# GpSimd in place of the sync queue for the turned blocks of h, with a reordered start and halved last sums, in a two-layer encoder kernel

## Chip, cores and metric

The kernel runs on one core of a Trainium2 chip. The metric is the device time of one execution in microseconds; lower is better. A core has five engines that run side by side, each through its own list of instructions in order: TensorE (PE; its weight loads are PEld), VectorE (DVE), ScalarE (ACT), GpSimd (POOL) and the sync engine (SP), which issues transfers. They meet through semaphores.

## The reference

Two layers over x of 256 rows by 1024 columns, in float32:

```python
for i in range(DEPTH):                       # 2
    h = rmsnorm(x, ffn1_norm[i])
    x = x + 0.5 * swiglu(h, ffn1_w_gate[i], ffn1_w_up[i], ffn1_w_down[i])
    h = rmsnorm(x, mix_norm[i])
    q_s, k_s, v_s, q_m = split(h @ w_in[i])
    o_m = memory_attention(q_m, *kv(rmsnorm(mem, mem_norm[i]) @ w_mem_kv[i]))
    o_s = chunked_rel_attention(...) if i % 2 == 0 else diff_attention(...)   # rotary in layer 1
    x = x + concat(o_s, o_m) @ w_out[i]
    h = rmsnorm(x, ffn2_norm[i])
    x = x + 0.5 * swiglu(h, ffn2_w_gate[i], ffn2_w_up[i], ffn2_w_down[i])
```

`swiglu(h, g, u, d)` is `(silu(h @ g) * (h @ u)) @ d`, with 2816 hidden columns. So there are four feed-forward blocks, two before and two behind a mixer.

## The kernel before

**Numbers.** Every large product is made of three TensorE products on float32r parts: high times high, low of the weights times high of the activations, high times low (`dense`, L378 to L392, products at L383, L386, L389). So each weight is split: ACT copies it to `hi` (L302), DVE subtracts to get `lo` (L314).

**Weights.** They come in chunks of 1 MB, 128 partitions by 2048 numbers. `loader` issues them on the sync queue (L270) into three `raw` buffers, `split_hi` and `split_lo` split a chunk in four quarters of 512 columns into four pairs of `hi` and `lo` buffers, and a `raw` buffer is free again when DVE has made the last `lo` of its chunk. A chunk of gate and up weights holds 512 rows by 256 columns of each; two chunks make a group, and 11 groups a feed-forward block.

**Activations.** The 256 rows are two row blocks (`tb` 0 and 1) of 128. `prep_half` turns half of a row block of x (`hf`): four transposes on TensorE (L396) into `xtp`, the gain times it on DVE (`y`, L427), the high part on ACT (`xh`, L430), the low part on DVE (`xl`, L432). The norm's factor is applied after the product.

**A feed-forward block** (`ffn`). For each group, 48 products give `gu` for both row blocks, in PSUM. `evac` makes silu on ACT (`sil`, L491), the product `h` on DVE (L494), and turns h: DVE transposes blocks of 32 by 32 (`hb`, L503), one transfer of 256 KB writes them to DRAM (`hd`, L508), and four of 64 KB read them back with the blocks in their new places (`hr`, L514). ACT and DVE then split `hr` into `ht` (L521, L523). The second half multiplies `ht` with the down weights into four PSUM sums (`acc`); `finish` adds them to x (L466). In the very last block it stores the sum to `out` (L473).

**What sets the order.** `Flow` simulates the engines in Python while the kernel is written out: each step waits for a modelled time or a free buffer, and the order in which the steps come due is the order in which instructions stand on each engine. A changed delay can so move instructions on every engine. On the chip each engine then runs its list in order and waits where an input isn't there; in particular a transfer on the sync queue that waits for its source holds up all transfers behind it.

**The start.** The sync queue loads the first gains and half of x's first row block, the first chunk in four pieces, then the other halves of x between weights. TensorE runs some `warm` products meanwhile. Four `start` threads turn the halves of x at written times (L1279).

Of the kernel before, what the change touches and what calls it, by code (L numbers as in the profile page):

```python
# [17 lines left out]
ALU = mybir.AluOpType  # L18
AX = mybir.AxisListType

P = 128
# [6 lines left out]
KT = D // P  # L28
# [114 lines left out]
def kernel(  # L143
# [10 lines left out]
    nc = tc.nc  # L154
    PSUM = bass.MemoryType.PSUM
    NRAW, NHL, NT2 = 3, 4, 19
    flow = Flow()
# [27 lines left out]
    def load_x(tb, hf):  # L185
        nc.sync.dma_start(out=xs[tb][:, hf * 512:(hf + 1) * 512],
                          in_=x[0, tb * P:(tb + 1) * P, hf * 512:(hf + 1) * 512])

    load_x(0, 0)

    ident = const.tile([P, P], F32, name="ident")
    make_identity(nc, ident)
# [56 lines left out]
    chunks = []  # L249
    raw_left = [NRAW]  # L250
    hl_left = [NHL]
    dma_free = [2.3]
    LAT = 1.5
    at = [0]

# [7 lines left out]
    def loader():  # L263
        for i, c in enumerate(chunks):
            yield lambda: raw_left[0] > 0
            raw_left[0] -= 1
            c.raw = wraw.tile([P, 2048], F32, tag="raw", name=f"raw{i}")
            dma_free[0] = max(dma_free[0], flow.now)
            for j, (dst, src) in enumerate(c.parts):
                nc.sync.dma_start(out=dst(c.raw), in_=src)  # L270
                dma_free[0] += 2.9 / len(c.parts)
                if j == 1 and i < 2:
                    c.early = dma_free[0] + LAT
                    if i:
                        load_x(1, 1)
                        dma_free[0] += 0.7
            c.arrive = dma_free[0] + LAT
            if i == 0:
                load_x(1, 0)
                load_x(0, 1)  # L280
                dma_free[0] += 1.4
            if i > 4 and late_done[0] < len(late_loads):
# [35 lines left out]
    def k4(t):  # L318
        return t.rearrange("p (k n) -> p k n", k=4)
# [140 lines left out]
    def finish(acc, tb, xt, gc, half):  # L460
        for hf in range(2):
            sl = slice(hf * 512, (hf + 1) * 512)
            yield lambda: acc.t[tb][hf] is not None
            yield acc.t[tb][hf]
            if half:
                nc.vector.scalar_tensor_tensor(out=xs[tb][:, sl], in0=acc.ps[tb][hf], scalar=0.5, in1=xs[tb][:, sl],  # L466
                                               op0=ALU.mult, op1=ALU.add)
            else:
                nc.vector.tensor_add(xs[tb][:, sl], acc.ps[tb][hf], xs[tb][:, sl])
            banks.give()  # L470
            yield flow.dve(512)
            if xt is None:
                nc.sync.dma_start(out=out[0, tb * P:(tb + 1) * P, sl], in_=xs[tb][:, sl])  # L473
            else:
                yield from prep_half(xt, tb, hf, gc)


    def ffn(l, nm, xt, gc_next):
# [3 lines left out]
        def evac(g, ps, end):  # L482


            hb = None
            for tb in range(2):
                yield lambda: end[tb] is not None and xt.rt[tb] is not None
                yield end[tb]
                yield g2.has(3)
                sil = g2.take([P, 256], F32, "sil")  # L490
                nc.scalar.activation(sil, ps[tb][:, 0:256], AF.Silu, scale=xt.r[tb])  # L491
                yield flow.act(256)
                h = g2.take([P, 256], F32, "h")
                nc.vector.scalar_tensor_tensor(out=h, in0=ps[tb][:, 256:512], scalar=xt.r[tb], in1=sil,  # L494
                                               op0=ALU.mult, op1=ALU.mult)
                t = flow.dve(256, 0.06)
                g2.give()
                banks.give()
                if hb is None:
                    hb = g2.take([P, 4, 2, 2, 32], F32, "hb")  # L500
                yield t
                for f in range(2):
                    nc.vector.transpose(out=hb[:, :, f, tb, :], in_=h[:, f * P:(f + 1) * P])  # L503
# [4 lines left out]
            nc.sync.dma_start(out=hd.rearrange("a i b x -> (a i) (b x)"), in_=hb.rearrange("p b f t j -> p (b f t j)"))  # L508
            yield flow.now + 3.0
            g2.give()  # L510
            yield g2.has()
            hr = g2.take([P, 4, 2, 2, 32], F32, "hr")
            for b in range(4):
                nc.sync.dma_start(out=hr[32 * b:32 * b + 32].rearrange("p a f t j -> p a (f t j)"),  # L514
                                  in_=hd[:, :, b, :].rearrange("a i x -> i a x"))
# [5 lines left out]
            nc.scalar.copy(out=hi, in_=src)  # L521
            yield flow.act(512)
            nc.vector.tensor_sub(lo, src, hi.bitcast(F32))  # L523
            t = flow.dve(512)
            g2.give()
            hts[g], htt[g] = ht, t

        for g, ids in enumerate(plan[l, nm, "gu"]):
            flow.until(banks.has(2))
            ps = [bank(f"gu{tb}", (P, 512)) for tb in range(2)]  # L530
            end = [None, None]
            flow.spawn(evac(g, ps, end))
            order = [(tb, c) for tb in range(2) for c in range(2)] if g == 0 and (l, nm) != (0, 1) else \
                    [(tb, c) for c in range(2) for tb in range(2)]
            for tb, c in order:
                for k in range(4):
                    kk = 4 * c + k
                    t = dense(ps[tb], xt.h[tb][:, kk, :], xt.l[tb][:, kk, :], lambda: xt.t[tb][kk], ids[c], k,
                              lambda w: k4(w)[:, k, :], kk == 0, kk == KT - 1)
                if c == 1:  # L540
                    end[tb] = t
        flow.until(banks.has(4))
        acc = Acc()
# [706 lines left out]
    xt = Xt()  # L1250

    def start_gain():
        tp = bank("gps0")
        nc.tensor.transpose(out=tp[:, 0, :16], in_=g1row, identity=ident[:16, :16])
        yield flow.pe(T_TR)
        nc.vector.tensor_copy(gcol[:, 0:16], tp[:, 0, :16])
        banks.give()
        flow.dve(16)
        warm(2)
        yield 5.0  # L1260
        warm(6)

    def start(tb, hf, t):
        yield t
# [11 lines left out]
    flow.spawn(start_gain())  # L1276
    for tb in range(2):
        for hf in range(2):
            flow.spawn(start(tb, hf, (3.75, 8.2, 7.4, 10.4)[2 * tb + hf]))  # L1279
    flow.spawn(gain_columns())  # L1280
    flow.spawn(rope_setup(), idle=True)
    flow.spawn(lambda_setup())
# [58 lines left out]
```

## Time and profile before

| | us |
|---|---|
| median of 3 runs | 974.63 |
| lowest, highest | 974.41, 975.08 |
| profiled execution | 975.12 |
| its span, from the first to the last instruction | 973.3 |
| busy in the span: PE, PEld, DVE, ACT, POOL | 964.6, 791.3, 675.7, 542.4, 60.1 |
| sync-queue issues: weights gate, up and down, hd, hr | 90, 90, 44, 44, 176 |

A line of the profile names the source line, the engine, the operation, what it writes and reads, and how many there are. A wait names who waited and whose semaphore ended it last. A matmul's end is modelled, so busy TensorE isn't TensorE at its peak; two products that follow each other overlap, and it is the distance of their starts that counts. "SPq" is the sync queue; the duration of a transfer on it is that of its issue, not of the bytes.

### The profile page before, as it was taken

What the parts mean: (1) busy time and instruction counts of PE and PEld (TensorE: products, weight loads), DVE (VectorE), ACT (ScalarE), POOL (GpSimd) and SP (SyncE); (2) the same over time, 40 slices, a digit from 0 to 9 for tenths busy, and PEclk for the clock granted to TensorE, in tenths of its full rate; (3) what the DMA queues carried; (4) which work ended last, traced back from release to release, by engine and by line L of the source; (5) the groups of instructions that cost most, each with busy time, mean ns of one, the idle gap of its engine ahead of it and who ended that gap; (6) DMA issues with size and microseconds to landing.
All of it is one profiled execution on the core that took longest, in us unless ns stands there. A gap on an engine that the chain in (4) does not pass through costs nothing.

```text
span 973.3 us, 13393 instructions
## 1 busy us (share of the span) xinstructions
PE 964.6 (99%) x4576; PEld 791.3 (81%) x4576; DVE 675.7 (69%) x1485; ACT 542.4 (56%) x1159; POOL 60.1 (6%) x65
## 2 busy tenths in 40 slices
PE   9999999999999999999999999999999999999998
PEld 7888888887777888888888888888787788888886
DVE  6776675887777866666476676644989886676641
ACT  6554544766685655445445555443677764555540
POOL 0000000022210000000000000000344100000000
PEclk9999999999999999999999999999999999999999
DMA  9989766475525567887648887764641369788641
GB/s 289 306 242 270 257 225 206 162 260 173 174 87 173 163 209 223 242 263 242 235 124 252 250 252 237 253 207 136 207 140 50 125 199 284 235 251 254 226 130 44
DMA packets 164447, 200.90 MB, mean 206 GB/s; under 512 B 9433, under 2 KB 140058, under 8 KB 164378
## 3 DMA queue, kind: packets, MB, share of 16 engines
q1 hardware_dynamic: 164378, 200.04, 65.5%
q8 instruction: 36, 0.59, 0.3%
q14 instruction: 33, 0.27, 0.1%
HBM read 187.42 MB, written 12.58 MB: 205 GB/s over the span
## 4 chain that ended last, share of the span: by engine, by line
PE 91%; DVE 5%; ACT 1%; DMA 1%; issue 0%; SPq 0%; ACTq 0%
PE gu L383 16%; PE gu L386 16%; PE gu L389 16%; PE acc L386 9%; PE acc L389 9%; PE acc L383 9%; PE pj L389 3%; PE pj L383 3%; PE pj L386 3%; DVE lo L314 2%; PE xtp L396 1%; PE S L983 1%; PE AV L1064 1%; PE kv L389 1%; PE kv L386 1%; PE kv L383 1%
## 5 line engine op out<-in xcount | busy, mean ns | idle before, releaser
L314 DVE TENSOR_TENSOR lo<-raw,hi 128x512 fp32r<-128x512 f32 x656 | 416.5, 684 | 161.5 <-ACT hi L302 161.3
L302 ACT CAST hi<-raw 128x512 fp32r<-128x512 f32 x656 | 365.4, 618 | 241.3 <-PE gu L389 117.9
L389 PE MATMUL gu<-hi,xl 128*128 128x512 f32 x704 | 274.3, 390 | 0.0
L383 PE MATMUL gu<-hi,xh 128*128 128x512 f32 x704 | 274.1, 389 | 0.0
L386 PE MATMUL gu<-lo,xh 128*128 128x512 f32 x704 | 274.0, 389 | 0.0
L389 PEld LDWEIGHTS gu<-hi,xl 128*128 128x128 f32 x704 | 132.2, 188 | 27.5
L383 PEld LDWEIGHTS gu<-hi,xh 128*128 128x128 f32 x704 | 132.2, 188 | 27.3
L386 PEld LDWEIGHTS gu<-lo,xh 128*128 128x128 f32 x704 | 132.2, 188 | 27.2
L383 PE MATMUL acc<-hi,ht 128*128 128x512 f32 x352 | 137.7, 391 | 0.0
L386 PE MATMUL acc<-lo,ht 128*128 128x512 f32 x352 | 137.3, 390 | 0.2 <-DVE lo L314 0.2
L389 PE MATMUL acc<-hi,ht 128*128 128x512 f32 x352 | 137.4, 390 | 0.0
L386 PEld LDWEIGHTS acc<-lo,ht 128*128 128x128 f32 x352 | 66.1, 188 | 14.1 <-DVE lo L314 0.7
L389 PEld LDWEIGHTS acc<-hi,ht 128*128 128x128 f32 x352 | 66.1, 188 | 13.7
L383 PEld LDWEIGHTS acc<-hi,ht 128*128 128x128 f32 x352 | 66.1, 188 | 13.5
L523 DVE TENSOR_TENSOR ht<-hr,ht 128x512 fp32r<-128x512 f32 x44 | 30.3, 688 | 55.0 <-ACT ht L521 55.0
L521 ACT CAST ht<-hr 128x512 fp32r<-128x512 f32 x44 | 27.1, 617 | 69.5 <-DMA hr<-hd 69.5
L389 PE MATMUL pj<-hi,xl 128*128 128x512 f32 x160 | 64.6, 404 | 0.0
L386 PE MATMUL pj<-lo,xh 128*128 128x512 f32 x160 | 63.6, 398 | 0.0
L383 PE MATMUL pj<-hi,xh 128*128 128x512 f32 x160 | 63.6, 398 | 0.0
L491 ACT ACTIVATE sil<-gu,xr 128x256 f32<-128x256 f32 x88 | 41.4, 470 | 17.5 <-PE gu L389 17.5
L503 DVE STREAM_TRANSPOSE hb<-h 128x128 f32<-128x128 f32 x176 | 44.1, 289 | 1.2
L494 DVE SCALAR_TENSOR_TENSOR h<-gu,xr,sil 128x256 f32<-128x256 f32 x88 | 42.2, 480 | 1.6
(167 smaller groups left out, 806.5 us busy)
## 6 DMA issues: line engine op xcount, KB each, us to landing
raw<-in_ffn_w_down_dram SPq DMA_DIRECT2D x44, 1024.0 KB
raw<-in_ffn_w_gate_dram SPq DMA_DIRECT2D x86, 512.0 KB
raw<-in_ffn_w_up_dram SPq DMA_DIRECT2D x86, 512.0 KB
raw<-in_w_in_dram SPq DMA_DIRECT2D x32, 512.0 KB
hd<-hb SPq DMA_DIRECT2D x44, 256.0 KB
hr<-hd SPq DMA_DIRECT2D x176, 64.0 KB
raw<-in_w_out_dram SPq DMA_DIRECT2D x8, 1024.0 KB
raw<-in_w_mem_kv_dram SPq DMA_DIRECT2D x4, 1024.0 KB
```

What stands on the lines that cost most here:

```text
L302: nc.scalar.copy(out=c.hi[:, sl], in_=c.raw[:, sl])
L314: nc.vector.tensor_sub(c.lo[:, sl], c.raw[:, sl], c.hi.bitcast(F32)[:, sl])
L383: nc.tensor.matmul(out=ps, lhsT=xh, rhs=wh, start=start, stop=False)
L386: nc.tensor.matmul(out=ps, lhsT=xh, rhs=wl, start=False, stop=False)
L389: nc.tensor.matmul(out=ps, lhsT=xl, rhs=wh, start=False, stop=stop)
L396: nc.tensor.transpose(out=dst, in_=src, identity=flip if flipped else ident)
L491: nc.scalar.activation(sil, ps[tb][:, 0:256], AF.Silu, scale=xt.r[tb])
L494: nc.vector.scalar_tensor_tensor(out=h, in0=ps[tb][:, 256:512], scalar=xt.r[tb], in1=sil, op0=ALU.mult, op1=ALU.mult)
L503: nc.vector.transpose(out=hb[:, :, f, tb, :], in_=h[:, f * P:(f + 1) * P])
L521: nc.scalar.copy(out=hi, in_=src)
L523: nc.vector.tensor_sub(lo, src, hi.bitcast(F32))
L983: nc.tensor.matmul(out=ss[e][:, pr, :nk], lhsT=q[rows, pr, :], rhs=k[rows, pr, :], start=i == 0, stop=i == len(passes) - 1)
```

## The change

Four edits:

1. The transfers `hd` and `hr` are issued by GpSimd instead of the sync queue.
2. At the start, x's second row block's first half is loaded ahead of the weights, both second halves behind the first chunk; the planned times of `start` change from (3.75, 8.2, 7.4, 10.4) to (3.75, 9.2, 4.6, 9.9); six `warm` products become ten, in pairs.
3. In the first group, the products go through the eight slices of the inner dimension and take both row blocks at each, where they took four slices of one row block and then of the other. All other groups keep their order.
4. The last feed-forward block adds its sums in 256-column pieces, and stores them in turn from the sync queue and from ACT.

```diff
     load_x(0, 0)
+    load_x(1, 0)
...
-    dma_free = [2.3]
+    dma_free = [4.0]
...
                 if j == 1 and i < 2:
                     c.early = dma_free[0] + LAT
-                    if i:
-                        load_x(1, 1)
-                        dma_free[0] += 0.7
...
             if i == 0:
-                load_x(1, 0)
                 load_x(0, 1)
+                load_x(1, 1)
...
+            if xt is None:
+                for q in range(2):
+                    qs = slice(hf * 512 + q * 256, hf * 512 + q * 256 + 256)
+                    nc.vector.scalar_tensor_tensor(out=xs[tb][:, qs], in0=acc.ps[tb][hf][:, q * 256:q * 256 + 256],
+                                                   scalar=0.5, in1=xs[tb][:, qs], op0=ALU.mult, op1=ALU.add)
+                    yield flow.dve(256)
+                    (nc.scalar if q else nc.sync).dma_start(out=out[0, tb * P:(tb + 1) * P, qs], in_=xs[tb][:, qs])
+                banks.give()
+                continue
...
-            nc.sync.dma_start(out=hd.rearrange("a i b x -> (a i) (b x)"), in_=hb.rearrange("p b f t j -> p (b f t j)"))
+            nc.gpsimd.dma_start(out=hd.rearrange("a i b x -> (a i) (b x)"), in_=hb.rearrange("p b f t j -> p (b f t j)"))
...
-                nc.sync.dma_start(out=hr[32 * b:32 * b + 32].rearrange("p a f t j -> p a (f t j)"),
+                nc.gpsimd.dma_start(out=hr[32 * b:32 * b + 32].rearrange("p a f t j -> p a (f t j)"),
...
+            if (l, nm) == (0, 1) and g == 0:
+                order = [(tb, kk) for kk in range(KT) for tb in range(2)]
...
-        yield 5.0
-        warm(6)
+        for t in (5.0, 5.6, 6.2, 6.8, 7.4):
+            yield t
+            warm(2)
...
-            flow.spawn(start(tb, hf, (3.75, 8.2, 7.4, 10.4)[2 * tb + hf]))
+            flow.spawn(start(tb, hf, (3.75, 9.2, 4.6, 9.9)[2 * tb + hf]))
```

Where instructions stand now. On TensorE at the start of the program, before (`x_85` and `x_86` are x's first and second row block, `gu_147` and `gu_148` their sums):

```order
L396 MATMUL xtp<-ident,x_85 128x128 x4
L1269 MATMUL warm<-ident 128x128 x6
L396 MATMUL xtp<-ident,x_86 128x128 x4
L383 MATMUL gu_147<-hi_166,xh_126 128x512
L386 MATMUL gu_147<-lo_167,xh_126 128x512
L396 MATMUL xtp<-ident,x_85 128x128 x4
L389 MATMUL gu_147<-hi_166,xl_128 128x512
L383 MATMUL gu_147<-hi_166,xh_126 128x512
```

and in the changed kernel, at the same place (its source lines differ by a few):

```order
L394 MATMUL xtp<-ident,x_85 128x128 x4
L394 MATMUL xtp<-ident,x_86 128x128 x4
L1277 MATMUL warm<-ident 128x128 x10
L381 MATMUL gu_147<-hi_178,xh_126 128x512
L384 MATMUL gu_147<-lo_179,xh_126 128x512
L387 MATMUL gu_147<-hi_178,xl_128 128x512
L394 MATMUL xtp<-ident,x_85 128x128 x4
L381 MATMUL gu_148<-hi_178,xh_127 128x512
L384 MATMUL gu_148<-lo_179,xh_127 128x512
L394 MATMUL xtp<-ident,x_86 128x128 x4
L387 MATMUL gu_148<-hi_178,xl_129 128x512
```

The first transposes of the second row block went ahead of the warm products, and the last transposes of both stand within the first two triples. On DVE at the start, before:

```order
L427 TENSOR_TENSOR y<-xtp,gcol 128x512
L432 TENSOR_TENSOR xl_128<-y,xh_126 128x512
L314 TENSOR_TENSOR lo_167<-raw_110,hi_166 128x512 x3
L427 TENSOR_TENSOR y<-xtp,gcol 128x512
L314 TENSOR_TENSOR lo_167<-raw_110,hi_166 128x512
```

and in the changed kernel:

```order
L425 TENSOR_TENSOR y<-xtp,gcol 128x512 x2
L430 TENSOR_TENSOR xl_128<-y,xh_126 128x512
L430 TENSOR_TENSOR xl_129<-y,xh_127 128x512
L312 TENSOR_TENSOR lo_179<-raw_111,hi_178 128x512 x4
L425 TENSOR_TENSOR y<-xtp,gcol 128x512 x2
```

Two instructions of the second row block, y and xl, now stand ahead of the first weight split. On the sync queue in the first block, before, around the first group's h:

```order
L508 DMA hd<-hb 128x512
L270 DMA raw_369<-in_ffn_w_gate_dram 128x4x256
L270 DMA raw_369<-in_ffn_w_up_dram 128x4x256
L285 DMA grow<-in_ffn_norm_dram 16x128
L514 DMA hr<-hd 32x4x128 x4
L270 DMA raw_400<-in_ffn_w_gate_dram 128x4x256
```

and in the changed kernel on POOL, from its first norm factors on:

```order
L401 TENSOR_TENSOR xr<-v,nhalf 128x1 x2
L512 DMA hd<-hb 128x512
L518 DMA hr<-hd 32x4x128 x4
L512 DMA hd<-hb 128x512
L518 DMA hr<-hd 32x4x128 x4
```

On POOL the transfers of all 11 groups of a block follow each other with no other instruction between them; on the sync queue only weights, x and small constants are left. Apart from these moves, the lists of all engines are the same in both kernels from the first block's fourth group to the last sums.

More of the change, by code (lines that the diff above doesn't have):

```diff
@@ L471, in finish @@
             yield flow.dve(512)
[L472 to L475, printed above, removed]
+            yield from prep_half(xt, tb, hf, gc)
     def ffn(l, nm, xt, gc_next):
@@ L532, in ffn @@
             flow.spawn(evac(g, ps, end))
[L533 to L540, printed above, removed]
+            if (l, nm) == (0, 1) and g == 0:
+                order = [(tb, kk) for kk in range(KT) for tb in range(2)]
+            elif g == 0:
+                order = [(tb, kk) for tb in range(2) for kk in range(KT)]
+            else:
+                order = [(tb, 4 * c + k) for c in range(2) for tb in range(2) for k in range(4)]
+            for tb, kk in order:
+                c, k = kk // 4, kk % 4
+                t = dense(ps[tb], xt.h[tb][:, kk, :], xt.l[tb][:, kk, :], lambda: xt.t[tb][kk], ids[c], k,
+                          lambda w: k4(w)[:, k, :], kk == 0, kk == KT - 1)
+                if kk == KT - 1:
                     end[tb] = t
```

## The prediction

> **What bounds the kernel now.** I read the page first, then the busy times by stretch, then who waits on TensorE and on the sync queue, and last the timeline at both ends. The page's engine line and six stretches (columns: length, then busy time and instruction count of PE, PEld, DVE, ACT, POOL, the granted clock, the DMA share and GB/s):
>
> ```profile
> PE 964.6 (99%) x4576; PEld 791.3 (81%) x4576; DVE 675.7 (69%) x1485; ACT 542.4 (56%) x1159; POOL 60.1 (6%) x65
> 0.00:9.00 9.00, 6.71 (x33) 6.26 (x34) 2.81 (x6) 4.08 (x7) 1.21 (x10) 1.00 0.70 215
> 12.30:160.00 147.70, 147.70 (x654) 121.99 (x653) 106.39 (x236) 82.33 (x161) 1.11 (x2) 1.00 0.84 262
> 330.00:480.00 150.00, 150.00 (x664) 124.24 (x663) 96.92 (x216) 75.34 (x148) 0.94 (x1) 1.00 0.77 238
> 510.00:660.00 150.00, 150.00 (x663) 124.25 (x662) 96.23 (x190) 76.31 (x144) 0.86 (x1) 1.00 0.78 239
> 690.00:780.00 90.00, 87.82 (x502) 69.29 (x502) 81.25 (x184) 64.69 (x182) 30.89 (x27) 1.00 0.40 130
> 800.00:950.00 150.00, 150.00 (x663) 124.20 (x663) 96.10 (x189) 76.29 (x145) 0.00 (x0) 1.00 0.73 228
> ```
>
> In the four feed-forward stretches TensorE is busy without a gap, at one product per 0.226 us (150 us by 663), while DVE has a third of its time free and ACT half. The h blocks are turned in exactly these stretches. TensorE loses time only at the start, around layer 1's mixer (690 to 780) and at the end. The waits on TensorE say the same, and those on the sync queue and on ACT show what the moved transfers hold up today (waiter, releaser, us in total, times, longest):
>
> ```profile
> PE xtp L396 <- DMA x<-in_x_dram: 0.9, 1, 0.9
> PE acc L386 <- DVE lo L314: 0.2, 1, 0.2
> SPq L270 <- DVE lo L314: 367.1, 115, 18.5
> SPq L508 <- DVE hb L503: 167.9, 39, 6.1
> SPq L514 <- DMA hd<-hb: 34.0, 25, 5.3
> ACT ht L521 <- DMA hr<-hd: 69.5, 26, 6.2
> ```
>
> The sync queue does stand still 201.9 us in all for the h transfers, with weight loads queued behind them. But no TensorE wait names a weight that landed late in those stretches: the loads have slack. How much, the counts of weight quarters split by DVE (L314) and of the middle products started (L386) give, each quarter serving two of these, at 420 us, the leanest place in them:
>
> ```profile
> 0.00:420.00 420.00, 180.76 (x284) 1.00 0.69 215
> ...
> 0.00:420.00 420.00, 216.87 (x553) 104.00 (x554) 1.00 0.69 215
> ```
>
> 284 less 553/2 is 7.5 quarters ahead; a quarter is six products, 1.36 us, so TensorE could run 10.2 us there with no new weight. That cover hides most of this change.
>
> **The h transfers, moved to GpSimd.** 44 groups lose 5 sync-queue issues each. The two rows of durations are min/median/max in ns; below them, the first group on the timeline, and the dearest group of POOL instructions today (busy us, mean ns):
>
> ```profile
> L514 SPq DMA_DIRECT2D hr<-hd x176: 312/427/1487, 30.8 to 916.5; - x176
> L508 SPq DMA_DIRECT2D hd<-hb x44: 338/345/506, 26.0 to 913.1; - x44
> ...
> 26.04 0.42 SPq L508 DMA_DIRECT2D hd<-hb  x1
> 30.77 1.77 SPq L514 DMA_DIRECT2D hr<-hd  x4
> 35.59 0.62 ACT L521 CAST ht<-hr 128x512 fp32r<-128x512 f32 x1 [2.89 <-DMA hr<-hd]
> ...
> L403 POOL TENSOR_TENSOR hf<-v,nhalf 128x8 f32<-128x8 f32 (+1 forms) x20 | 30.9, 1544 | 106.1 <-DVE v L401 88.0 <-DVE sst L450 18.0
> ```
>
> The sync queue is freed of 176 times 0.427 and 44 times 0.345, 90 us of issuing, besides the 201.9 us of waiting. Gain on the path: nothing, since its weight loads then wait for the next thing, a raw buffer that DVE frees (the 367.1 us row), and TensorE already has them early. No stretch without a TensorE gap can become shorter by it, and layer 1's mixer holds no h transfer.
>
> The cost sits on the other side. What waits now on POOL is hd for hb, and hr for hd's landing; queued behind are only the next group's five transfers, since POOL computes nothing in these stretches but one or two reciprocal roots (0 to 2 instructions in the four rows above). What waits for POOL is ACT's ht, and behind it in ACT's order the next weight splits. The trace shows no GpSimd transfer, so I bound its issue by the sync queue's 0.35 us from below and POOL's dearest group, 1.54 us, from above, and take 1.0 between them; below the sync queue's price a gain would again find nothing to shorten. A group then holds POOL for 1.0 for hd, its landing (26.46 to 30.77, 4.3 us, behind a megabyte of weights in the same queue; shorter if the new queue is served in turn), and 4.0 for hr: 9.3 us, within the 10.9 us that TensorE gives a group (48 products of 0.226). POOL keeps up; ht comes 2.8 us later than today (5.0 of issues for 2.2), and the 10.2 us of lead hide that. Without that lead it would cost up to 2.8 us in each of 44 groups. I put 0, with ends 0 and the first rival below.
>
> One row speaks against so calm a view: DVE is busy 96.92 us of the 150 in the second stage, mostly with instructions of 0.68 us, beside every one of these issues. The Trainium skill (SBUF — State Buffer, SBUF: two separate sides) warns that GpSimd cannot write a transfer's descriptors while DVE holds the port that the two share, as it does in certain copy modes. The same page clears a two-input subtraction, which is most of DVE's work here, of holding the write side; no run here shows either. If the warning held for all of DVE's work, each issue would wait out the instruction in hand, and the sum would change as in the second rival; by the rows alone it stays at 0.
>
> **The start.** Columns: start, duration, engine, line, what.
>
> ```profile
> 4.59 1.06 PE L396 MATMUL xtp<-ident,x 128*128 128x128 f32 x4
> 5.68 0.69 DVE L427 TENSOR_TENSOR y<-xtp,gcol 128x512 f32<-128x512 f32 x1 [1.83 <-PE xtp L396]
> 6.41 0.62 ACT L430 CAST xh<-y 128x512 fp32r<-128x512 f32 x1 [4.19 <-DVE y L427]
> 6.93 2.18 ACT L302 CAST hi<-raw 128x512 fp32r<-128x512 f32 x4
> 7.06 0.69 DVE L432 TENSOR_TENSOR xl<-y,xh 128x512 fp32r<-128x512 f32 x1 [0.68 <-ACT xh L430]
> 7.67 1.89 DVE L314 TENSOR_TENSOR lo<-raw,hi 128x512 fp32r<-128x512 f32 x3
> 8.59 0.66 PE L396 MATMUL xtp<-ident,x 128*128 128x128 f32 x4 [0.94 <-DMA x<-in_x_dram]
> 9.01 0.48 PE L383 MATMUL gu<-hi,xh 128*128 128x512 f32 x1
> 9.33 0.40 PE L386 MATMUL gu<-lo,xh 128*128 128x512 f32 x1
> 9.60 0.42 PEld L396 LDWEIGHTS xtp<-ident,x 128*128 128x128 f32 x4 [0.32 <-DMA x<-in_x_dram]
> 11.95 0.60 PE L396 MATMUL xtp<-ident,x 128*128 128x128 f32 x4
> 15.37 0.39 PE L389 MATMUL gu<-hi,xl 128*128 128x512 f32 x1
> ```
>
> Today the first product stands behind transposes that wait for x of the second row block (8.59). The 24th and last product of the first chunk starts at 15.37, and from about 12.6 on there is no gap, so this is where a gain would show. In the new order that x block lands before the weights, and the block's y, xh and xl go ahead of the first split. Worked through with the rows' spacing (0.21 us between early transposes, 0.60 between DVE's and 0.52 between ACT's 512-wide instructions): the four extra transposes take 0.85 us, so the second y starts at 6.53 and ends at 7.22; its xh on ACT runs 7.25 to 7.87; hi follows, 7.77 to 8.39; on DVE the second xl runs 7.9 to 8.6 and the first lo to 9.2. The first lo product comes at 9.25, against 9.33. So the wait for x (0.9 us) goes and a longer chain through DVE and ACT stands in its place. After it: the third product at 9.48, four transposes of the next x block (the same bytes lie ahead of it as today, so it lands by 9.60) to 10.13, two products, the last x block's transposes at 10.6 (a block later: 8.59 to 9.60 is one block) to 11.03, then products alone: the 24th at 11.03 + 18 x 0.226 = 15.1. Gain 0.26 us.
>
> Ends: 0.7 us gained if lo goes as soon as hi is there, 8.5; 0.9 us lost if the last x block still lands at 11.9 as today. Later chunks are covered: each quarter of the first chunk is now used by both row blocks in turn, so demand for splits is slower, and the second chunk is wanted at 15.3.
>
> **The end.** The last sums, their store, and a 128x256 sum of the same kind (page, mean 480 ns):
>
> ```profile
> 969.57 0.69 DVE L466 SCALAR_TENSOR_TENSOR x<-acc,x 128x512 f32<-128x512 f32 x1 [3.39 <-PE acc L389]
> 970.28 0.33 SPq L473 DMA_DIRECT2D out_dram<-x  x1
> ...
> 971.00:972.00 1.00, 0.00 (x0) 0.00 (x0) 0.00 (x0) 0.00 (x0) 0.00 (x0) 1.00 0.70 262
> ...
> L494 DVE SCALAR_TENSOR_TENSOR h<-gu,xr,sil 128x256 f32<-128x256 f32 x88 | 42.2, 480 | 1.6
> ```
>
> The last 256 KB flow within 971 to 972 (262 GB/s), then come the receipt and the span's end at 973.3. Two half sums end by 969.57 + 0.40 + 0.48 = 970.45 (if they overlap by 0.08, as DVE's back-to-back instructions do), 0.19 later than the one; the last store is then half as large, 0.5 us less, with the other half already under way. Net 0.3 gained, 0.5 if the sums cost no more than the one. ACT issues no transfer today; at the sync queue's 0.33 the gain stands, at its slowest hr issue, 1.49, it is a loss of 0.9; I take 0.33, the like transfer. The six other half sums hide beside TensorE, as the four stores do now.
>
> **The sum.** 0 - 0.26 - 0.3 is -0.56 us. The profiled execution took 975.12 us (973.3 of span and 1.8 around it), 0.05% above the median of 974.63; taken from its own time that gives 974.56, and on the median's footing 974.1 us. The measurement can tell about 0.2%, 1.95 us, from no change, so this is no change.
>
> **The rivals.** *POOL falls behind by its own price (slower).* If a GpSimd issue costs 1.6 us, just over POOL's dearest row, a group takes 1.6 + 4.3 + 6.4 = 12.3 us of POOL against 10.9 of TensorE; it slips 1.4 us a group, 14 us by a stage's eleventh, past the lead of 10.2 us in the leanest stage: some 4 us of TensorE gap, 978.1 us, and steeply more beyond. The deciding point is 1.3 us an issue, where a group fills 10.9. For it: no row bounds the issue. Against: the dearest row is arithmetic, and the landing should shrink in a queue without weights. Chance 0.05.
>
> *DVE holds GpSimd off (slower).* An issue of 1.0 that first waits out a DVE instruction of 0.68 takes 1.68; a group takes 5 x 1.68 + 4.3 = 12.7, slips 1.8, 18 us by the eleventh, 8 past the leanest lead: 982 us. For it: DVE is busy 65% of the stretch. Against: a third of the issues would find it idle, which brings the mean to 1.44 and the slip to 6 us, inside the lead. Chance 0.04.
>
> *Earlier weights shorten layer 1's mixer, or the start gains its full 0.7 and more (faster).* The chain of waits holds one weight transfer at the mixer's end:
>
> ```profile
> 767.22 6.30 DMA raw<-in_ffn_w_up_dram
> ```
>
> Landing 3 us sooner would give 971.1. Against: no h transfer is queued there, and the buffer that it waits for comes from DVE. Chance 0.11 for all that ends under 972.7.
>
> *The end or start turns (slower).* Both worst ends, 0.9 and 0.9, give 976.4, still no change; with something around the span for the two new queues it could pass 976.6. Chance 0.03.
>
> **How the numbers follow.** The forecast, within 0.2%, has the remaining 0.77; slower has 0.05 + 0.04 + 0.03. The range is the forecast's: down by the start's further 0.45, the end's 0.2 and the runs' own spread of 0.35 to 973.0, up by the start's worst end against the forecast (1.15) and half of the end's (1.2) to 975.8, since both worst together are unlikely; the far rivals stay outside.
>
> **What would show it.** Right: the four feed-forward stretches of the new trace keep a PE without gaps, L314's count stays 6 quarters or more ahead, sync-queue waits for hb are gone and those for lo grow; the first lo product at about 9.2 and the 24th at about 15.1. Wrong: a TensorE wait for lo or ht in those stretches, POOL issues above 1.3 us, or a first chunk that ends after 15.8; a gain above 2 us would have to appear between 690 and 780, where I expect none.

## The result and the profile after

The changed kernel takes 1037.11 us (median of 6 runs, 1035.75 to 1041.80) against 974.77 us for the kernel before in the same comparison (6 runs, 974.41 to 975.08). The ratio is 1.0646, with an interval of 1.0626 to 1.0666: 62.3 us slower, where 974.1 us and no change were forecast. The profiled execution of the changed kernel has a span of 1034.9 us.

The engine line of the page after, and the first feed-forward stretch (columns as in the prediction); below them the counts of weight quarters split by DVE (L312) and of middle products started (L384) up to 160 us:

```profile
PE 985.7 (95%) x4584; PEld 796.9 (77%) x4584; DVE 670.2 (65%) x1489; ACT 534.8 (52%) x1159; POOL 181.0 (17%) x285
12.30:160.00 147.70, 140.53 (x605) 114.36 (x603) 87.87 (x192) 69.17 (x139) 28.66 (x52) 0.98 0.73 222
...
0.00:160.00 160.00, 63.93 (x102) 0.98 0.73 225
...
0.00:160.00 160.00, 80.31 (x204) 38.77 (x204) 0.98 0.73 225
```

Before, TensorE was busy through the whole of 12.3 to 160 us and started 654 products in it. Now it starts 605 in the same time: 49 fewer, and at 0.226 us each that is 11 us lost by 160 us alone. The busy time hides much of this (140.53 of 147.70), the count of products shows it. DVE and ACT are less busy than before in this stretch, and the DMA share fell from 0.84 to 0.73. So something waits, everywhere a little, and no engine is saturated. The lead of weights is gone: 102 quarters less 204/2 is 0, where the prediction asked for 6 or more.

A part of the loss shows in the granted clock. In the changed kernel it is 0.5 in four stretches (79.4 to 86.2, 195.5 to 202.3, 683.6 to 687.0 and 932.8 to 939.6 us), each behind gaps in TensorE's work. The 46 products that start in them stand 0.43 us apart (median) instead of 0.226, an estimate of at most 9 us. The kernel before has no such stretch until its last product is done.

Who waits, from the waits of the changed kernel (waiter, releaser, us in total, times, longest):

```profile
POOL hd L512 <- DVE hb L507: 337.0, 44, 10.8
ACT ht L525 <- DMA hr<-hd: 317.0, 44, 10.5
DVE ht L527 <- ACT ht L525: 251.7, 43, 9.4
PE acc L381 <- ACT hi L300: 16.4, 10, 5.2
PE gu L381 <- ACT hi L300: 7.9, 6, 2.2
PE acc L384 <- DVE lo L312: 6.1, 11, 0.7
PE gu L384 <- DVE lo L312: 5.9, 9, 0.7
```

ACT's `ht` waited 69.5 us in 26 groups before; it waits 317.0 us in all 44 now, and DVE's `ht` another 251.7 us behind it. TensorE waits for weight halves `hi` and `lo`, which the prediction named as the sign that it is wrong. Yet POOL isn't the late one: it waits 337.0 us for `hb`, in every group. Everybody waits for somebody else in the same circle, and the circle has to be followed. The price of an issue, and how long the bytes take from issue to landing (line, engine, operation, count, busy us, mean ns; then count, KB each, median us):

```profile
L518 POOL DMA_DIRECT2D hr<-hd x176 | 95.7, 550 | 124.8 <-ACT hi L300 59.8
L512 POOL DMA_DIRECT2D hd<-hb x44 | 25.0, 569 | 337.0 <-DVE hb L507 337.0
L312 DVE TENSOR_TENSOR lo<-raw,hi 128x512 fp32r<-128x512 f32 x656 | 412.7, 682 | 37.9 <-ACT hi L300 37.3
...
hd<-hb POOLq DMA_DIRECT2D x44, 256.0 KB, 2.5
hr<-hd POOLq DMA_DIRECT2D x176, 64.0 KB, 6.0
```

Issues cost 0.55 and 0.57 us, near the lower end of the prediction's bounds and not the 1.0 taken. DVE's instructions take what they took. But a piece of `hr`, a quarter of the bytes of `hd`, lands 6.0 us after its issue. The page before gives no landing for the sync queue.

**The circle.** DVE's list around one group, the same in both kernels (the names are those of the changed one; `h` of the group's second row block, then the low half of `ht` of the group before, then `hb`):

```order
L498 SCALAR_TENSOR_TENSOR h<-gu_5054,xr,sil 128x256
L527 TENSOR_TENSOR ht<-hr,ht 128x512
L507 STREAM_TRANSPOSE hb<-h 128x4x32 x2
```

DVE takes its list in order, so the `hb` of group g can't be made before the `ht` of group g-1 is. That `ht` needs ACT's `ht`, that needs `hr` to land, that needs `hd` to land, and that needs the `hb` of group g-1. The chain starts at an `hb` and comes back to the next `hb`. One turn in the changed kernel, on the timeline (start, duration, engine, line, what, idle time before and who ended it):

```profile
602.32 0.50 DVE L507 STREAM_TRANSPOSE hb<-h 128x128 f32<-128x128 f32 x2
603.11 0.56 POOL L512 DMA_DIRECT2D hd<-hb  x1 [8.10 <-DVE hb L507]
606.12 2.17 POOL L518 DMA_DIRECT2D hr<-hd  x4 [2.44 <-ACT hi L300]
608.43 0.48 DVE L498 SCALAR_TENSOR_TENSOR h<-gu,xr,sil 128x256 f32<-128x256 f32 x1
614.37 0.62 ACT L525 CAST ht<-hr 128x512 fp32r<-128x512 f32 x1 [7.79 <-DMA hr<-hd]
615.02 0.69 DVE L527 TENSOR_TENSOR ht<-hr,ht 128x512 fp32r<-128x512 f32 x1 [6.11 <-ACT ht L525]
615.63 0.50 DVE L507 STREAM_TRANSPOSE hb<-h 128x128 f32<-128x128 f32 x2
```

`h` of the second row block is ready at 608.91, and its `hb` waits until 615.63 for the `ht` that stands ahead of it, though `hb` uses nothing of it. From `hb` to `hb` is 615.63 - 602.32 = 13.31 us, and the legs fill it without slack: 0.79 to the issue of `hd`, 0.56 for that, 2.45 until POOL issues `hr`, 2.17 for the four issues, 6.08 until ACT can read `hr`, 0.65 and 0.61 through ACT and DVE. TensorE needs 10.88 us a group (48 products of 0.226).

The same turn before:

```profile
592.81 0.50 DVE L503 STREAM_TRANSPOSE hb<-h 128x128 f32<-128x128 f32 x2
593.33 0.34 SPq L508 DMA_DIRECT2D hd<-hb  x1
595.43 1.75 SPq L514 DMA_DIRECT2D hr<-hd  x4
602.24 0.61 ACT L521 CAST ht<-hr 128x512 fp32r<-128x512 f32 x1
603.69 0.50 DVE L503 STREAM_TRANSPOSE hb<-h 128x128 f32<-128x128 f32 x2
```

From `hb` to `hb` is 10.88 us, TensorE's own period, and `ht` has no waiting time in brackets: the circle is there, but it is shorter than the period and has some slack. Over the 44 groups the chain from the end of `hb` to the start of ACT's `ht` is 11.9 us on average after and 9.2 before, ACT's own order and waiting included. With the 1.8 us of `ht` on ACT, `ht` on DVE and `hb` (0.62, 0.69, 0.50) the circle is 13.7 us after. Before it is at most 11.0, next to the period, and the transfers alone are done earlier than that: the last packet of `hr` is through 8.0 us after `hb` on average, and ACT waits for `hr` in only 26 groups.

An estimate of the loss from this: 13.3 - 10.9 = 2.4 us in each of the 11 groups of a block is 26 us; the lead of 10.2 us that the prediction read off covers part of it; 16 us are left, and four blocks make 64 us. Measured: 62.3. That the two come so near is partly luck. From the first gate product to the last down product the four blocks are 20.8, 9.5, 15.4 and 16.5 us longer than before; these add up to the loss, but no block is the average one.

### The profile page after: what moved, and what is told of

It is laid out like the page before. It is cut to its first block, busy times and chain, and to the rows that moved or that the text cites. A ratio compares the mean times of both kernels' runs of the same rounds, so it can differ in the third digit from the quotient of the medians.

```text
span 1034.9 us, 13443 instructions
## 1 busy us (share of the span) xinstructions
PE 985.7 (95%) x4584; PEld 796.9 (77%) x4584; DVE 670.2 (65%) x1489; ACT 534.8 (52%) x1159; POOL 181.0 (17%) x285
## 5 line engine op out<-in xcount | busy, mean ns | idle before, releaser
L312 DVE TENSOR_TENSOR lo<-raw,hi 128x512 fp32r<-128x512 f32 x656 | 412.7, 682 | 37.9 <-ACT hi L300 37.3
L300 ACT CAST hi<-raw 128x512 fp32r<-128x512 f32 x656 | 360.8, 617 | 80.9 <-PE gu L387 30.3
L381 PE MATMUL gu<-hi,xh 128*128 128x512 f32 x704 | 276.9, 393 | 7.9 <-ACT hi L300 7.9
L384 PE MATMUL gu<-lo,xh 128*128 128x512 f32 x704 | 276.9, 393 | 5.9 <-DVE lo L312 5.9
L527 DVE TENSOR_TENSOR ht<-hr,ht 128x512 fp32r<-128x512 f32 x44 | 30.4, 692 | 251.7 <-ACT ht L525 251.7
L525 ACT CAST ht<-hr 128x512 fp32r<-128x512 f32 x44 | 27.3, 620 | 317.0 <-DMA hr<-hd 317.0
L384 PEld LDWEIGHTS gu<-lo,xh 128*128 128x128 f32 x704 | 133.3, 189 | 36.9 <-DVE lo L312 8.8
L381 PE MATMUL acc<-hi,ht 128*128 128x512 f32 x352 | 140.8, 400 | 16.4 <-ACT hi L300 16.4
L384 PE MATMUL acc<-lo,ht 128*128 128x512 f32 x352 | 140.2, 398 | 6.1 <-DVE lo L312 6.1
L387 PE MATMUL acc<-hi,ht 128*128 128x512 f32 x352 | 139.0, 395 | 0.0
L518 POOL DMA_DIRECT2D hr<-hd x176 | 95.7, 550 | 124.8 <-ACT hi L300 59.8
L384 PEld LDWEIGHTS acc<-lo,ht 128*128 128x128 f32 x352 | 67.0, 190 | 24.6 <-DVE lo L312 10.8
L512 POOL DMA_DIRECT2D hd<-hb x44 | 25.0, 569 | 337.0 <-DVE hb L507 337.0
L387 PEld LDWEIGHTS acc<-hi,ht 128*128 128x128 f32 x352 | 67.0, 190 | 13.3
L384 PE MATMUL pj<-lo,xh 128*128 128x512 f32 x160 | 63.6, 398 | 0.0
L401 POOL TENSOR_TENSOR hf<-v,nhalf 128x8 f32<-128x8 f32 (+1 forms) x20 | 30.9, 1545 | 108.5 <-DVE v L399 88.3
```

What stands on the lines that cost most here:

```text
L300: nc.scalar.copy(out=c.hi[:, sl], in_=c.raw[:, sl])
L312: nc.vector.tensor_sub(c.lo[:, sl], c.raw[:, sl], c.hi.bitcast(F32)[:, sl])
L381: nc.tensor.matmul(out=ps, lhsT=xh, rhs=wh, start=start, stop=False)
L384: nc.tensor.matmul(out=ps, lhsT=xh, rhs=wl, start=False, stop=False)
L387: nc.tensor.matmul(out=ps, lhsT=xl, rhs=wh, start=False, stop=stop)
L401: nc.gpsimd.tensor_tensor(out=dst, in0=v[:, :n], in1=nhalf[:, :n], op=ALU.pow)
```

## The experiments

The theory under test: the loss comes from the length of this circle (call it the ring) alone; what lengthens it costs, what shortens it or opens it doesn't. The rivals: GpSimd as an issuer is too slow or disturbs the engines beside it, whatever the order; the wait that counts is that of ACT, which splits the weights; the other three edits have a part in it.

**Which edit.** The first kernel is the one before with only `hd` and `hr` moved; the second is the changed kernel with only these two moved back, the same lines the other way round.

```diff
-            nc.sync.dma_start(out=hd.rearrange("a i b x -> (a i) (b x)"), in_=hb.rearrange("p b f t j -> p (b f t j)"))
+            nc.gpsimd.dma_start(out=hd.rearrange("a i b x -> (a i) (b x)"), in_=hb.rearrange("p b f t j -> p (b f t j)"))
...
-                nc.sync.dma_start(out=hr[32 * b:32 * b + 32].rearrange("p a f t j -> p a (f t j)"),
+                nc.gpsimd.dma_start(out=hr[32 * b:32 * b + 32].rearrange("p a f t j -> p a (f t j)"),
```

Expected of the first: 

> Edit: the kernel before with the first edit alone, hd and hr issued from GpSimd; start, first products and last sums as before. Ring theory: on DVE the list reads h of group g, ht of group g-1, hb of group g, so hb(g) waits for ht(g-1), which waits for the transfers that hb(g-1) started; on GpSimd that ring is 11.6 us of transfers and 1.8 of ACT and DVE work, 13.4 us against the 10.9 that TensorE takes for a group, so all of the loss is here: 1036 to 1038 us. Queue theory (the GpSimd queue's own traffic slows weights or DVE): also about 1037. Rival, the new start and last sums carry the loss: 975.

Expected of the second: 

> Edit: the changed kernel with hd and hr back on the sync queue, so the reordered start and the halved last sums alone. Ring and queue theories alike: no loss, 974.1 us by the prediction's own sum for the start and the end (0.26 and 0.3 gained on 974.8 to 974.6). Rival, these edits carry the loss: above 1000.

Measured: 1039.55 us (ratio 1.0636, 1.0612 to 1.0661), a little above the 1036 to 1038 expected, and 975.49 us (0.9995, 0.9986 to 1.0004). The transfers carry the whole loss, the other edits none of it.

**Opening the ring by order.** Nothing is made faster here: `ht` is planned 4 us later, so that it stands behind the next `hb` on DVE. From the changed kernel, ahead of `ht`:

```diff
-            yield flow.now + 4.0
+            yield flow.now + 8.0
```

Expected: 

> Edit: the changed kernel, transfers on GpSimd, with the planned delay between hr and ht raised from 4 to 8 us, which puts ht of group g-1 behind hb of group g on DVE and behind two more weight splits on ACT. Ring theory: the ring is cut, a chain of 13.4 us is then hidden, 974 to 977 us. Queue theory: the traffic is the same, so the loss stays, 1030 or more.

Measured: 974.22 us (973.74 to 974.35), ratio 0.9982 (0.9973 to 0.9991). 62.9 us come back with every transfer still on GpSimd at the same issue price. DVE's list and the timeline of this kernel:

```order
L498 SCALAR_TENSOR_TENSOR h<-gu_5054,xr,sil 128x256
L312 TENSOR_TENSOR lo_5147<-raw_5049,hi_5146 128x512
L507 STREAM_TRANSPOSE hb<-h 128x4x32 x2
L312 TENSOR_TENSOR lo_5147<-raw_5049,hi_5146 128x512
L527 TENSOR_TENSOR ht<-hr,ht 128x512
```

```profile
593.48 0.56 POOL L512 DMA_DIRECT2D hd<-hb  x1 [5.28 <-DVE hb L507]
597.35 2.17 POOL L518 DMA_DIRECT2D hr<-hd  x4 [3.31 <-ACT hi L300]
603.57 0.50 DVE L507 STREAM_TRANSPOSE hb<-h 128x128 f32<-128x128 f32 x2
604.76 0.62 ACT L525 CAST ht<-hr 128x512 fp32r<-128x512 f32 x1 [1.50 <-DMA hr<-hd]
605.41 0.69 DVE L527 TENSOR_TENSOR ht<-hr,ht 128x512 fp32r<-128x512 f32 x1 [0.77 <-ACT ht L525]
...
12.30:160.00 147.70, 147.70 (x652) 121.99 (x651) 106.23 (x235) 82.92 (x160) 31.39 (x57) 1.00 0.84 261
```

The chain from `hd` to `ht` is as long as ever (593.48 to 604.76, 11.3 us). But `hb` now comes before `ht`, the next turn has begun by then, and TensorE is back at 652 products without a gap.

**On which engine the ring closes.** The edit above moves `ht` on ACT too. This one moves only DVE's half, and leaves ACT to wait for `hr` where it did. From the changed kernel, between the two halves of `ht`:

```diff
-            yield flow.act(512)
+            yield flow.act(512) + 1.5
```

Expected: 

> Edit: the changed kernel, all h transfers on GpSimd, with 1.5 us more of planned delay between ht's two halves, so that on DVE the low half of ht(g-1) comes behind hb(g), while the high half keeps its place on ACT, ahead of the same weight splits. Ring theory (the ring closes on DVE): 974 to 982 us. Rival, ACT standing still for ht in front of weight splits is enough by itself: 1020 or more.

Measured: 976.31 us (974.02 to 977.35), ratio 1.0005 (0.9994 to 1.0016). The wait that looked worst after DVE's, ACT's for `hr`, is still there in large part:

```profile
ACT ht L525 <- DMA hr<-hd: 138.2, 36, 9.3
```

138.2 us of it cost nothing against the kernel before that the interval shows. They may not be wholly free: the interval lies above that of `e3_late_ht`, and in this trace the first block's gate and up products take 123.7 us, against 121.4 there and 121.1 before. But the loss of 62 us is gone with DVE's half of `ht` alone, so the ring closes through DVE's list.

**A longer chain without GpSimd.** If it is length that counts, the sync queue must show the same loss when the chain gets an extra hop: `hd` is copied to a second buffer in memory, and `hr` reads that. This adds 256 KB a group read and written. From the changed kernel with `hd` and `hr` back on the sync queue:

```diff
+            hd2 = dram.tile([4, 32, 4, P], F32, tag="hd2", name="hd2")
+            nc.sync.dma_start(out=hd2.rearrange("a i b x -> (a i) (b x)"), in_=hd.rearrange("a i b x -> (a i) (b x)"))
...
-                                  in_=hd[:, :, b, :].rearrange("a i x -> i a x"))
+                                  in_=hd2[:, :, b, :].rearrange("a i x -> i a x"))
```

Expected: 

> Edit: as the kernel with the start and last sums alone (all h transfers on the sync queue), with one more transfer of 256 KB, hd copied to a second buffer in DRAM, between hd and hr. Ring theory: no GpSimd in it, but the ring grows by an issue and a landing, about 2.3 us, from 10.2 to 12.5, over 10.9: slower by 10 to 35 us, 985 to 1010. Queue theory: no GpSimd traffic, no loss beyond a few us, 974 to 977.

Measured: 1019.38 us (1013.4 to 1022.9), ratio 1.0422 (1.0391 to 1.0453). The kind of loss is the expected one, without a single transfer on GpSimd; ACT's `ht` again waits in nearly every group:

```profile
ACT ht L527 <- DMA hr<-hd: 291.4, 43, 9.7
```

The size was missed: I expected 985 to 1010. The hop adds more than the 2.3 us that I gave it: from the end of `hd`'s issue to the first `hr` it is 5.6 us on average, against 2.6 in `e2_rest_only`, and the ring takes this in each of 44 groups.

**How much of the chain.** From the changed kernel, one of the two transfers goes back to the sync queue, first `hr`:

```diff
-                nc.gpsimd.dma_start(out=hr[32 * b:32 * b + 32].rearrange("p a f t j -> p a (f t j)"),
+                nc.sync.dma_start(out=hr[32 * b:32 * b + 32].rearrange("p a f t j -> p a (f t j)"),
```

and in another kernel `hd`:

```diff
-            nc.gpsimd.dma_start(out=hd.rearrange("a i b x -> (a i) (b x)"), in_=hb.rearrange("p b f t j -> p (b f t j)"))
+            nc.sync.dma_start(out=hd.rearrange("a i b x -> (a i) (b x)"), in_=hb.rearrange("p b f t j -> p (b f t j)"))
```

Expected of `hd` alone: 

> Edit: the changed kernel with hr back on the sync queue, hd alone on GpSimd. From the traces, hd on GpSimd adds 0.3 of start, 0.2 of issue and 0.6 of landing: 1.1 us. Ring theory: 10.2 + 1.1 = 11.3 us, 0.4 over a group of 10.9, 4 us a block, inside the lead: 974 to 980 us. A theory that any GpSimd transfer costs: half of the loss, about 1005.

Expected of `hr` alone: 

> Edit: the changed kernel with hd back on the sync queue, hr alone on GpSimd. hr on GpSimd adds 0.3 of start, 0.4 of issue and 1.9 of landing: 2.6 us. Ring theory: 12.8 us, 1.9 over a group, 21 us a block less some 12 of lead, four times: 995 to 1020 us. A theory by which only both together cost: about 975.

Measured: `hd` alone 974.90 us (0.9999, 0.9990 to 1.0008), `hr` alone 1016.16 us (1.0424, 1.0410 to 1.0439). ACT's `ht` in the two, `hd` alone first:

```profile
ACT ht L525 <- DMA hr<-hd: 20.8, 14, 5.9
```

```profile
ACT ht L525 <- DMA hr<-hd: 303.8, 43, 10.0
```

The 1.1 us that `hd` alone was expected to add don't show: its chain is 9.0 us on average, and it costs nothing. `hr` alone takes the ring past the period.

The traces of all these kernels, side by side: the mean from the end of `hb` to ACT's `ht`, the mean turn from `hb` to the next group's `hb` within a block, and the median time less that of the kernel before in the same comparison, all in us.

| kernel | `hb` to ACT's `ht` | turn | loss |
|---|---|---|---|
| `hd` on GpSimd | 9.0 | 10.9 | -0.4 |
| before | 9.2 | 11.0 | 0 |
| two of four `hr` on GpSimd (below) | 10.2 | 11.8 | 3.4 |
| `hr` on GpSimd | 11.5 | 13.1 | 40.9 |
| extra hop, all on the sync queue | 11.7 | 13.2 | 44.1 |
| changed | 11.9 | 13.5 | 62.3 |
| before, with `hd` and `hr` on GpSimd | 11.9 | 13.6 | 64.2 |
| changed, late `ht` | 11.3 | 10.9 | -1.1 |

In all rows but the last the turn is the chain and its 1.8 us of work, to within 0.4 us, and the loss rises with the chain, whichever queue made it long. Near the period it is free; above it every group pays. In the last row the ring is open: the chain and the work, 13.1 us, are longer than the turn, and nothing is lost.

**What makes `hr` slow on GpSimd.** Either each piece takes 6 us for itself, or the four pieces go one behind the other. Two of the four back on the sync queue tell them apart. From the changed kernel:

```diff
-                nc.gpsimd.dma_start(out=hr[32 * b:32 * b + 32].rearrange("p a f t j -> p a (f t j)"),
+                (nc.gpsimd if b < 2 else nc.sync).dma_start(out=hr[32 * b:32 * b + 32].rearrange("p a f t j -> p a (f t j)"),
```

Expected: 

> Edit: the changed kernel with two of the four hr transfers of a group on GpSimd and two on the sync queue; ht at its old place. In the trace of the changed kernel the four hr are issued 0.54 us apart, but their packets come about 1.4 us apart. If GpSimd works through them one by one (piece theory), two of them land 2.8 us sooner, the ring is 10.6 us: 974 to 980 us. If a GpSimd transfer has a fixed long landing, only two issues, 1.1 us, go, the ring is 12.3: 985 to 1005.

Measured: 978.31 us (977.7 to 980.6), ratio 1.0041 (1.0025 to 1.0056).

```profile
hr<-hd SPq DMA_DIRECT2D x88, 64.0 KB, 4.8
hr<-hd POOLq DMA_DIRECT2D x88, 64.0 KB, 5.1
```

Had each piece taken its 6 us whatever goes beside it, the time would have been 985 or more; it fell by 59 us. So the pieces delay each other. The changed kernel says the same: issues are 0.54 us apart, but the first to the fourth piece of a group land 4.3, 5.5, 6.7 and 6.5 us after their issue (medians of 44), and in one group the packets of the four begin at 635.16, 637.07, about 637.6 and about 639.2, the last at 640.4.

But 6.0 us isn't a fixed price of GpSimd's queue. On the sync queue the pieces of the kernel with the extra hop land after 4.3 us, and in `e3_late_ht`, on GpSimd at the same issue price, after 3.7:

```profile
hr<-hd SPq DMA_DIRECT2D x176, 64.0 KB, 4.3
...
hr<-hd POOLq DMA_DIRECT2D x176, 64.0 KB, 3.7
```

What differs is when they are issued and what else then moves: around the group above, from 632 to 641 us, the weights' queue alone takes 81% of the DMA engines' time. How much of the 6.0 us is the queue and how much the weights isn't separated here. DVE isn't the reason: in the turn shown it stands idle for 6.11 us while the pieces are on their way. The remaining 0.4% lies in the first block, whose gate and up products take 125.3 us in this trace against 121.1 before; the other three are as before.

**Late `ht` elsewhere.** Does the later `ht` bring something of itself, without GpSimd? First in the kernel before, then in the changed one with everything on the sync queue, beside a repeat of the fastest version. The edit is the one that opened the ring:

```diff
-            yield flow.now + 4.0
+            yield flow.now + 8.0
```

Expected in the kernel before: 

> Edit: the kernel before, all on the sync queue, with the planned delay between hr and ht raised from 4 to 8 us. Ring theory: before had a ring of 10.2 us under 10.9, TensorE lost nothing to it, so cutting it gains nothing: within 0.2% of before. Rival, the ring cost before something too: faster by over 0.2%.

Expected with the new start: 

> Edit: the kernel of the late ht with hd and hr back on the sync queue, so new start, halved last sums, delay of 8 us, no GpSimd transfer. Ring theory: with the ring cut the queue of the h transfers doesn't matter, so this is within 0.2% of the same kernel with GpSimd and of before: 973.5 to 975.5 us; the 3.5 us that the late ht lost in the kernel before came from its start and don't show here. Rival, the late ht itself costs on the sync queue: 977 or more.

Expected of the repeat: 

> Edit: the kernel of the late ht with GpSimd again, beside the one on the sync queue. Ring theory: 974.2 us as before, within 0.2% of the sync-queue twin. Rival, the freed sync queue is worth something once the ring is cut: over 0.2% below the twin.

Measured: 978.73 us (977.35 to 979.81; ratio 1.0036, 1.0024 to 1.0049), 977.53 us (974.18 to 979.03; 1.0014, 0.9998 to 1.0030) and 974.23 us (973.78 to 974.72; 0.9991, 0.9982 to 1.0000). The first two are slower than expected. The repeat takes the 974.2 us expected, but that is 0.34% below its twin on the sync queue, where at most 0.2% was expected. The first one's trace puts most of its loss (3.2 of 4.7 us) ahead of any ring, at the start, where the 24th product begins at 18.58 us instead of 15.37. The one wait of TensorE for x in it, and three stretches of its start:

```profile
PE xtp L396 <- DMA x<-in_x_dram: 2.4, 1, 2.4
...
8.00:10.00 2.00, 0.00 (x0) 0.00 (x0) 1.18 (x3) 0.95 (x3) 0.00 (x0) 1.00 0.95 305
10.00:12.00 2.00, 1.66 (x8) 1.36 (x9) 1.43 (x3) 1.12 (x4) 0.00 (x0) 0.73 1.08 391
12.00:14.00 2.00, 2.00 (x8) 1.71 (x7) 1.62 (x3) 1.57 (x4) 0.00 (x0) 0.50 1.09 349
```

TensorE stood still for 2.4 us until x came, and then ran at a granted clock of 0.73 and 0.50 in these stretches. Neither the later `ht` nor another order can be the cause within these microseconds: the first `ht` comes at 38.7 us, and up to there every engine's list is that of the kernel before. `e1_h_only`, with the same old start, shows the same (24th product at 18.18). The kept trace of the kernel before doesn't, but 4 of its 21 executions beside this one took 977.4 to 978.7 us. Why x comes late in some executions stays open, and so does why all five of this kernel took 977.4 or more.

The second, at 977.53 us, reached the 977 that its rival named (the late `ht` itself costs on the sync queue). Nine of its ten executions lie above all eleven of the repeat. On the sync queue the later `ht` also moves `hd` and `hr` among the weights, and `hd` then lands 7.5 us after its issue (median), against 3.4 in the repeat; the chain there is 13.8 us. The kept trace is one of its faster executions (975.28), so it doesn't show what the slower ones lose. So `e3_late_ht` is the fastest version measured, by 0.18% and in the repeat 0.09%, the second at the edge of its interval. With the late `ht`, GpSimd's queue is the better of the two by 3.3 us; whether that is the freed sync queue or the new order on it isn't shown.

## Why the prediction was wrong

**What bounds the kernel** was read rightly: TensorE's 0.226 us a product, and a lead of some 10 us of weights. The place at 420 us isn't quite the leanest: at 398 us the same counts are 267 and 521, 6.5 quarters or 8.8 us.

**The step that failed** is in the part on the h transfers: "ht comes 2.8 us later than today, and the 10.2 us of lead hide that." The size came out right by luck: measured, the chain grew by 2.7 us (11.9 against 9.2). The prediction put all of it on the price of issues; of the 2.7, issues make 0.6, and 1.8 lie between the last issue of `hr` and ACT's `ht`. Hiding it behind a lead is right for a delay that comes once. This one comes in each of the 11 groups, because DVE's list ties each `hb` to the `ht` before it, so that group g+1 starts late by what group g lost. At 2.4 us a group, 10.2 us last four groups, and a block has eleven. The prediction even had the price, "up to 2.8 us in each of 44 groups", up to 123 us, and set it aside because the lead stood between.

What was missing was a row that needed no run: DVE's list of the kernel before has the three lines shown above in that order. The prediction followed forwards what waits for POOL ("ACT's ht, and behind it … the next weight splits"), and stopped there; `hb` of the next group is among those that wait behind `ht`, and with that the chain is closed. The traced turn of before, 10.88 us with a chain of 8.9 (593.31 to 602.24) and 1.8 of work, would have shown how near the ring is to the period.

**"POOL keeps up"** was right, with more room than thought. In the turn shown a group holds POOL for 0.56, 2.45 of landing and 2.17, or 5.2 us, not 9.3. The issue was taken at 1.0 us and is 0.55; the deciding point of 1.3 us was never near. The 4.3 us of landing was that of the first group, behind its weights; over all 44 groups it is 2.5 on average in the kernel before, from the end of `hd`'s issue to the first `hr`, and 2.7 after, so it didn't shrink. The time from the last issue of `hr` to ACT's `ht` grew, from 4.3 to 6.0 us on average, and no term held it: the sum had a price for issuing and none for the time from `hr`'s issue to its landing.

**No gain from a free sync queue** holds within what was called no change, between `e3_late_ht`, 974.22 us without the 90 us of issues on that queue, and `e2_rest_only`, 975.49 us with them: 0.13% apart. Between the two kernels with the late `ht` it is 0.34%, 974.23 against 977.53 us, which is more; its cause is open, as said above.

**The Trainium skill's warning** (SBUF — State Buffer, SBUF: two separate sides), which stood behind the second rival, is about copy modes, and the same page of the Trainium skill clears the two-input subtraction that is most of DVE's work here. The trace agrees with that: issues take 0.55 us beside DVE, and DVE's subtractions 682 ns against 684 before. Another page of the Trainium skill does bear on the surprise. DMA: Bandwidth & Descriptors (Anatomy of one DMA) gives a transfer from GpSimd a fixed 2.0 us and a rate; for the 256 KB of `hd` that is an estimate of 2.6 us and the trace has 2.5, but for 64 KB of `hr` it is 2.2 and the trace has 6.0 (3.7 in `e3_late_ht`, where `hd` has 3.3). `hr` moves in rows of 512 bytes, `hd` in rows of 2 KB, but no run here varies the row, so that this is the reason isn't shown. By bytes alone the Trainium skill's figure doesn't reach it, and the measurement decides.

**The start:** 0.26 us were forecast, the 24th product at 15.1. In `e2_rest_only` it begins at 15.09, in the changed kernel itself at 15.39, in `e3_late_ht` at 15.29, against 15.37 before. In the other kernels with the new start it lies between 14.80 and 15.97. The working holds in one execution, and the term is smaller than what executions differ by. Rows of the changed kernel:

```profile
9.46 0.39 PE L384 MATMUL gu<-lo,xh 128*128 128x512 f32 x1
...
10.83 0.60 PE L394 MATMUL xtp<-ident,x 128*128 128x128 f32 x4
```

The first `lo` product comes at 9.46, not 9.25, and the last x block's transposes at 10.83, not 10.6; they do not wait until 11.9 as before.

**The end:** 0.3 us were forecast; none came. In `e2_rest_only`:

```profile
968.81 0.39 PE L387 MATMUL acc<-hi,ht 128*128 128x512 f32 x1
969.24 0.76 DVE L466 SCALAR_TENSOR_TENSOR x<-acc,x 128x256 f32<-128x256 f32 x2 [3.32 <-PE acc L387]
969.69 0.33 SPq L469 DMA_DIRECT2D out_dram<-x  x1
970.02 0.34 ACTq L469 DMA_DIRECT2D out_dram<-x  x1
```

The sums take 0.76 together and ACT's issue 0.34, each within 0.12 of what was taken. The last product starts 4.09 us before the span's end at 972.9, against 4.16 before (969.14 to 973.3), and 4.20 in the changed kernel. From the start of the last store's issue to the span's end it is 2.88 us (970.02 to 972.9), against 3.02 before (970.28 to 973.3): halving the last store was to save 0.5 us and saved 0.14, and the two sums take 0.07 more than the one did.

**The rivals** had the right side with 0.12, and the wrong mechanism. "POOL falls behind" and "DVE holds GpSimd off" both slip per group against the lead, which is the right arithmetic (1.4 and 1.8 us a group, against 2.4 measured), but let POOL's own occupation be the circle. POOL in fact waits for `hb`. No rival turned the latency into a period.

## What to carry to other kernels

Before a step is called hidden by a lead, follow its result from engine to engine, through what merely stands behind it in an in-order list, until the chain ends or returns to the start of the next round. If it returns, compare its length with the round's period: below it a delay is free, above it each round pays and a lead only puts off the bill. Then cut the ring where it is cheapest, often by moving a waiting instruction behind one that doesn't need it, before or instead of making any leg faster.

## What the runs showed of the hardware

- A GpSimd transfer issue takes 0.55 to 0.57 us here, against 0.35 to 0.43 on the sync queue.
- GpSimd's four transfers of 64 KB in rows of 512 bytes, issued 0.54 us apart, land 6.0 us after issue (median) in the changed kernel, the later ones later (4.3, 5.5, 6.7 and 6.5 us); in `e3_late_ht` the same four land after 3.7 us. The 256 KB in rows of 2 KB land after 2.5 us in the one and 3.3 in the other.
- After 2.4 us without a product at the start of one execution, TensorE's granted clock was 0.73 in the next 2 us and 0.50 in the 2 us after. In the changed kernel it is 0.5 for 3.4 or 6.8 us four times, each behind gaps in TensorE's work.
